# Longer planned delays for the recurrence's steps, and a rearranged tail, in a three-branch mixer layer

## The chip, the core and the metric

The kernel runs on one core of a Trainium2 chip. It is one launch, and the metric is the device time of that launch in microseconds (us), the median of several runs. A core has a matrix engine (TensorE, PE; its weight loads are PEld), three elementwise engines (VectorE, DVE; ScalarE, ACT; GpSimd, POOL), and SyncE (SP), from whose queue this kernel issues its DMA transfers. Each engine takes its instructions in the order in which the program has them; semaphores make one engine wait for another.

## The reference

One layer of a diffusion backbone on 256 latent tokens and 256 context tokens, width 2048; only the latent stream is returned.

```python
h = rms_norm(x) * (1 + scale) + shift                  # context and latent rows, (512, 2048)
(na_q, na_k, na_v, na_gate, pool_u, pool_gate, rw_r, rw_k, rw_v, rw_gate,
 rw_lw, rw_la, merge_logits) = split(h @ w_in)         # w_in: 2048 x 16512
y_na   = neighbourhood_attention(q, k, v, k_ctx, v_ctx, rpb)    # 16 heads of 64
y_pool = multiscale_pool(pool_u)                       # windows 2, 4, 8, 16
y_rw   = rwkv7 over context, then latents, both directions      # 16 heads of 64
def step(S, inp):                                      # the recurrence of one head
    S = S * w + (S @ a) b^T + v k^T;  y = S @ r
b_i = y_i * silu(gate_i)                               # three branches, 1024 wide
merged = sum_i sigmoid(merge_logits_i) * (b_i @ w_branch[i])
out = rms_norm(x + gate * (merged @ w_out)) * final_g
```

All is float32. The kernel makes each large product from two halves of each operand, high and low, in three matmuls.

## The kernel before

**Stages.** First come the modulation, the norm and the first column tiles of `w_in` ("start"). Then a long mixed stage runs everything up to the branch products. The last stage ("out", matmuls named `o`) multiplies by `w_out`, adds the residual and stores.

**Filler work.** The mixed stage draws its large matmuls from units. A column tile (line L815, accumulator `d`) multiplies `h`, held in `hh0..15` and `hl0..15` (high and low), with 128 columns of `w_in`. A merge group (L582 to L584, accumulator `dg`) computes 512 columns of merge logits; there are 12, each of 8 units. A branch group (also `dg`) computes 512 columns of one branch's product in 4 units; there are 12: branches 0 (attention), 1 (pool) and 2 (recurrence), four each. Each unit loads one `raw` tile of weights (three buffers, L564); ACT casts its halves (`whi`, L576) and DVE subtracts the rest (`wlo`, L577). Entries of the list `todo` carry the name of an event that must have happened; merge groups carry none and so fill whatever is left.

**Small streams.** Beside the units run generators: attention and pooling (`side`), and `rwkv(p)` for each of eight head pairs p (two heads of 64; called "head p" from here on). A head goes through these steps:

- `features`, for q = 0 (context) and q = 1 (latents): matmuls `psw`, `psa`, `psn`, and much elementwise work that ends in the tile `BK` (L210, L211)
- `scores`: transposes `pv`, copied by ACT to `SV` (L235); transposes `pt` (L242) of `BK`, copied by ACT to `BKT` (L244); products `pb` and `pk` (L257, L259), masked by DVE into `AT` and `EO` (L277)
- `inverse`: the triangular blocks go through DRAM (`dA`, `iA`, `dT`, `AT`), 31 steps on DVE, and `merge`: DVE transposes `DN` (L335), matmuls `mp` (L339, L347)
- `chain`: eight chunk steps, each `px` (L374), then `pu` (L388), copied to `SV` (L390), then `pS` (L398)
- `readout`: `pm`, `pvv`, a square root, a reciprocal; then the gate `grwg`, and `keep`, which splits the result (`kh`, L843, and L845) and writes it to `bs` in DRAM (L846, L847)

`branch_load(i)` reads 256 rows of `bs` back as `bh{i}` and `bl{i}` (L623) into the place of `hh{i}`, `hl{i}`: i = 0 to 3 for attention, 4 to 7 for pool, 8 to 11 for the recurrence. The modulation's own gate is computed in 64 small loads `wg` (L1070) with matmuls `mg` (L1082), taken one at a time beside the units once attention and pooling have ended (`side7`).

**What sets the order.** The class `Order` keeps a planned clock `t`. A generator yields a pair: the planned PE time of what it has just issued, and a delay; it is taken up again when `t` has passed the delay, and filler units go in between. PE's instructions stand in just the order that this planning gives. The other engines' orders are set by the framework's scheduler. A longer delay issues nothing: it puts more filler matmuls between two steps.

```python
s.t += r[0]
x[1] = (s.t if r[0] else min(x[1], s.t)) + r[1]     # when the stream may go on
```

## Time and profile before

| | |
|---|---|
| median of 3 runs | 1622.84 us (1619.48 to 1625.39) |
| the profiled execution | 1622.48 us; its span, first to last instruction, 1620.7 us |
| mean granted clock of TensorE | 0.980 |
| HBM read, written | 265.38 MB, 21.50 MB |
| chain of work that ended last | PE 57%, DMA 6%, DVE 4%, ACT 3% of the span |

The profile is of one execution. In its rows, "PE pt L242 <- DVE BK L210: 7.0, 3, 2.9" says that PE sat idle before a `pt` of line 242 until DVE's `BK` of line 210 was done: 7.0 us in total, three times, the longest 2.9. Busy shares are means over stages with different limits, so the prediction goes by stages. "Clock" is the share of full speed that TensorE was granted.

### The profile page before, as it was taken

The page shows a single profiled execution, that of the slowest core. Times are in us where ns is not written, and L with a number is a line of the kernel's source. Part 1 is how long each engine was busy: PE and PEld are TensorE (multiplying, and loading weights), DVE is VectorE, ACT ScalarE, POOL GpSimd, SP SyncE. Part 2 cuts the span into 40 slices and gives each one's busy share as a digit, 9 for nine tenths or more (in the row PEclk, how much of TensorE's full clock was granted, in tenths as well). Part 3 has the DMA queues.
Part 4 walks back from the last instruction along what each step waited for, and adds up shares of the span by engine and source line. Part 5 has one row for each costly group of instructions (what it writes and reads, how often), then busy time and mean ns, then how long its engine had stood idle before and what let it go on. Part 6 is the DMA issues. An engine that isn't in the chain of part 4 may idle for free.

```text
span 1620.7 us, 32318 instructions
## 1 busy us (share of the span) xinstructions
PE 1532.6 (95%) x12280; PEld 1219.3 (75%) x12280; DVE 1125.8 (69%) x2566; ACT 809.4 (50%) x1603; POOL 241.9 (15%) x441
## 2 busy tenths in 40 slices
PE   6999989989999998998999999999898997999998
PEld 4667778778777887876887798788687664667787
DVE  4234887898787788778867778886786542556674
ACT  5224753674565465456445646645643342334553
POOL 2222100330130041031013014102203200000000
PEclk9999999999999999999999999999999998999999
DMA  9997355345443444622532554443265678899862
GB/s 375 331 331 235 121 161 169 119 140 163 118 134 104 141 148 137 182 94 80 180 118 81 157 158 126 139 128 110 63 198 170 191 253 281 286 288 307 284 234 103
DMA packets 218380, 289.26 MB, mean 178 GB/s; under 512 B 62576, under 2 KB 176368, under 8 KB 213616
## 3 DMA queue, kind: packets, MB, share of 16 engines
q1 hardware_dynamic: 218224, 287.20, 54.8%
q8 instruction: 96, 1.57, 0.4%
q14 instruction: 60, 0.49, 0.1%
HBM read 265.38 MB, written 21.50 MB: 177 GB/s over the span
## 4 chain that ended last, share of the span: by engine, by line
PE 57%; DMA 6%; DVE 4%; ACT 3%; issue 1%; SPq 0%; ACTq 0%; DVEq 0%
PE d L815 24%; PE dg L582 6%; PE dg L583 5%; PE dg L584 5%; PE o L582 2%; PE o L584 2%; PE o L583 2%; DMA raw<-in_w_br 2%; PE pu L388 1%; DMA wg<-in_w_mg 1%; PE px L374 1%; DMA bh<-bs 1%; PE pS L398 1%; PE mg L1082 1%; DVE wlo L577 1%
## 5 line engine op out<-in xcount | busy, mean ns | idle before, releaser
L576 ACT CAST whi<-raw 128x512 fp32r<-128x512 f32 x584 | 354.8, 619 | 420.3 <-PE d L815 188.8
L577 DVE TENSOR_TENSOR wlo<-raw,whi 128x512 fp32r<-128x512 f32 x584 | 401.3, 700 | 191.0 <-ACT whi L576 147.7
L815 PE MATMUL d<-hh,whi 128*128 128x256 f32 (+1 forms) x1184 | 370.5, 332 | 0.0
L815 PE MATMUL d<-hl,whi 128*128 128x256 f32 (+1 forms) x1184 | 360.7, 324 | 0.0
L815 PEld LDWEIGHTS d<-hh,whi 128*128 128x128 f32 x1184 | 226.5, 191 | 23.2 <-issue 1.8
L815 PE MATMUL d<-hh,wlo 128*128 128x256 f32 (+1 forms) x1184 | 243.0, 325 | 0.0
L815 PEld LDWEIGHTS d<-hl,whi 128*128 128x128 f32 x1184 | 226.9, 192 | 17.1 <-issue 0.9
L815 PEld LDWEIGHTS d<-hh,wlo 128*128 128x128 f32 x1184 | 184.0, 192 | 16.8 <-issue 0.7
L582 PE MATMUL dg<-whi,hh 128*128 128x512 f32 x384 | 165.8, 432 | 6.3 <-ACT whi L576 2.2
L584 PE MATMUL dg<-wlo,hh 128*128 128x512 f32 x384 | 152.7, 398 | 1.9 <-DVE wlo L577 1.9
L583 PE MATMUL dg<-whi,hl 128*128 128x512 f32 x384 | 152.7, 398 | 0.0
L370 POOL TENSOR_SCALAR sg<-SV,G 64x64 f32<-64x64 f32 x192 | 108.2, 569 | 225.6 <-DVE SV L405 128.9
L582 PEld LDWEIGHTS dg<-whi,hh 128*128 128x128 f32 x384 | 73.0, 190 | 30.4 <-issue 6.3
L582 PE MATMUL dg<-whi,bh 128*128 128x512 f32 x192 | 81.6, 425 | 8.3 <-ACT whi L576 4.7
L584 PEld LDWEIGHTS dg<-wlo,hh 128*128 128x128 f32 x384 | 73.4, 191 | 19.5 <-DVE wlo L577 2.7
L583 PEld LDWEIGHTS dg<-whi,hl 128*128 128x128 f32 x384 | 73.5, 191 | 10.6 <-issue 0.2
L584 PE MATMUL dg<-wlo,bh 128*128 128x512 f32 x192 | 76.4, 398 | 0.5 <-DVE wlo L577 0.5
L583 PE MATMUL dg<-whi,bl 128*128 128x512 f32 x192 | 76.2, 397 | 0.0
L309 DVE TENSOR_TENSOR iM<-iA,iT 128x126 f32<-128x126 f32 (+22 forms) x248 | 65.7, 265 | 8.4 <-DMA iA<-dA 2.4
L311 DVE TENSOR_TENSOR iT<-iT,iM 128x126 f32<-128x126 f32 (+22 forms) x248 | 65.7, 265 | 6.1
L748 ACT ACTIVATE hh<-xT,md 128x256 fp32r<-128x256 f32 x32 | 17.5, 593 | 90.9 <-DVE md L705 90.9
L582 PEld LDWEIGHTS dg<-whi,bh 128*128 128x128 f32 x192 | 36.6, 191 | 29.4 <-ACT whi L576 11.7
(323 smaller groups left out, 2514.9 us busy)
## 6 DMA issues: line engine op xcount, KB each, us to landing
raw<-in_w_in SPq DMA_DIRECT2D x244, 512.0 KB, 3.5
wm<-in_w_ms SPq DMA_DIRECT2D x32, 1024.0 KB, 6.8
raw<-in_w_br SPq DMA_DIRECT2D x48, 512.0 KB, 6.0
wg<-in_w_mg SPq DMA_DIRECT2D x64, 256.0 KB, 5.4
raw<-in_w_out SPq DMA_DIRECT2D x32, 512.0 KB, 4.3
wst<-in_w_st SPq DMA_DIRECT2D x16, 448.0 KB, 7.5
md__79<-mth SPq DMA_DIRECT2D x24, 256.0 KB, 3.0
bth<-md__79 SPq DMA_DIRECT2D x24, 256.0 KB, 3.8
```

The lines of the kernel that those rows point to most:

```text
L309: nc.vector.tensor_tensor(m, A[:, st:st + 1, st + 1:32].to_broadcast([128, ni, nt]), T[:, 0:ni, st:st + 1].to_broadcast([128, ni, nt]), AL ...
L311: nc.vector.tensor_tensor(T[:, 0:ni, st + 1:32], T[:, 0:ni, st + 1:32], m, ALU.add)
L370: nc.gpsimd.tensor_scalar(sg[hv[par], d], SV[hv[par], par, w, d], G[hv[par], gs[d][0], d:d + 1], None, ALU.mult)
L374: nc.tensor.matmul(px[hv[par], d], EO[:, par, d, cs[d], :], SV[:, par, w, d], start=True, stop=True, tile_position=(0, 64 * par))
L388: nc.tensor.matmul(pu[hv[par], d], AT[hv[par], cs[d], d, :], xs[hv[par], d], start=True, stop=True)
L576: nc.scalar.copy(hi, src)
L577: nc.vector.tensor_tensor(lo, src, hi.bitcast(F32), ALU.subtract)
L582: nc.tensor.matmul(acc, a[0], b[0], start=start, stop=False)
L583: nc.tensor.matmul(acc, a[1], b[0], start=False, stop=False)
L584: nc.tensor.matmul(acc, a[0], b[1], start=False, stop=stop)
L748: nc.scalar.activation(hh[j][:, c], xT[:, j, c], AF.Identity, bias=mds[j][:, e:e + 1], scale=mds[j][:, 2 + e:3 + e])
L815: nc.tensor.matmul(box[0], w[m >= 8][:, 128 * i:128 * i + 128], x, start=(v == 0 and m == 0), stop=(v == 3 and m == 11))
```

## The change

It has four parts.

1. Longer delays. Old and new, in planned us: after `psw`, `psa` 1.6 to 2.2; before `kk` 3.6 to 4.4; after `BK` 3.6 to 5.2 (q = 0) and 4.8 to 6.6 (q = 1); after `pv` 1.2 to 2.4; after `pt` 1.6 to 2.4; after each pair of `pb`, `pk` 2.6 to 3.4; after `DN` 2.8 to 4.4; after `mp` 1.8 to 2.4 and 1.6 to 2.2; after `px` 1.2 to 1.6 (q = 0) and 0.7 to 1.0 (q = 1); after `pu` 1.6 to 2.0; after `pS` 1.8 to 2.0 and 1.9 to 2.2; after `pm` 4.0 to 5.0.
2. The gate of head 7 (`rwg7`) may be computed once attention of head 7 has ended (event `at7`), into the buffer `g2n` of attention's gates; before, it waited for head 6's result and used `g2r`.
3. The last entry of `todo`, merge group 11, is held back until it is the only one.
4. The loads of branch inputs 0 to 7 go out one pair at a time, at units 5, 6, 7, 8, 10, 12, 14 and 16 counted from that last group's start, where before two pairs went out at each of units 4 to 7. Those of the recurrence go one at a time from unit 18 on, once head 7 is done. The gates' loads come with two of three halves of a unit (before: one of two), but not during units 4 to 8.

```diff
             (nc.scalar.copy if par else nc.vector.tensor_copy)(SV[hv[par], par, w], pu[hv[par]])
-            yield 0.4, 1.6
+            yield 0.4, 2.0
...
-            todo.append((f"rw{p - 1}" if p else None, gate_(RW_G + p, f"rwg{p}", "g2r")))
+            if p < 7:
+                todo.append((f"rw{p - 1}" if p else None, gate_(RW_G + p, f"rwg{p}", "g2r")))
+            else:
+                todo.append(("at7", gate_(RW_G + p, f"rwg{p}", "g2n")))
...
                             i = next((i for i, (ev, _) in enumerate(todo) if ev is None or O.has(ev)), None)
+                            if i is not None and i == len(todo) - 1 and todo[:-1]:
+                                i = None
...
                         if last is not None:
-                            for i in (2 * last - 8, 2 * last - 7):
-                                if 0 <= i < 8:
-                                    branch_load(i)
-                            if last >= 10 and loads and O.has("rw7"):
-                                branch_load(loads.pop(0))
+                            if last in (5, 6, 7, 8, 10, 12, 14, 16):
+                                branch_load(last - 5 if last < 9 else last // 2 - 1)
+                            if last >= 18 and loads and O.has("rw7"):
                                 branch_load(loads.pop(0))
                             last += 1
...
-                    if n % 2 and O.has("side7") and gates:
+                    if n % 3 and O.has("side7") and gates and not 4 <= (last or 0) < 9:
                         ready[-1] = ready[-1] + gates.pop(0)()
```

What that does to the order, at three places. First PE, from head 7's last `pt` of its context half to its first `pb`. In the names, `d15` is a column tile and `dg0` a merge group, `pu6_4` the fifth chain step of head 6. Before:

```order
L242 MATMUL pt7_0_1_13997<-ident_63,BK7_0_13728 128x64
L388 MATMUL pu6_4_14016<-xs6_4_13989,AT6_1_12707 64x64 x4
L815 MATMUL d15_13896<-hh8_89,whi593_13892 128x512
L815 MATMUL d15_13896<-hl8_105,whi593_13892 128x512
L815 MATMUL d15_13896<-hh9_90,whi593_13892 128x512
L815 MATMUL d15_13896<-hl9_106,whi593_13892 128x512
L815 MATMUL d15_13896<-hh10_91,whi593_13892 128x512
L815 MATMUL d15_13896<-hl10_107,whi593_13892 128x512
L257 MATMUL pb7_0_0_14035<-EO7_0_13947,BK7_0_13728 64x64 x2
```

The same stretch of PE now:

```order
L242 MATMUL pt7_0_1_15135<-ident_63,BK7_0_14839 128x64
L582 MATMUL dg0_15058<-whi689_15054,hh2_83 128x512
L583 MATMUL dg0_15058<-whi689_15054,hl2_99 128x512
L584 MATMUL dg0_15058<-wlo689_15055,hh2_83 128x512
L388 MATMUL pu6_4_15165<-xs6_4_15127,AT6_1_13626 64x64 x4
L582 MATMUL dg0_15058<-whi690_15062,hh3_84 128x512
L583 MATMUL dg0_15058<-whi690_15062,hl3_100 128x512
L584 MATMUL dg0_15058<-wlo690_15063,hh3_84 128x512
L582 MATMUL dg1_15106<-whi689_15054,hh2_83 128x512
L583 MATMUL dg1_15106<-whi689_15054,hl2_99 128x512
L584 MATMUL dg1_15106<-wlo689_15055,hh2_83 128x512
L257 MATMUL pb7_0_0_15182<-EO7_0_15080,BK7_0_14839 64x64 x2
```

Nine large matmuls stand in the gap where six stood, and the filler is a merge group: the place has moved from among the column tiles to the tail.

Second SP's queue around the loads of branch inputs. Before (`raw` are the weights of a unit, `wg` those of the modulation's gate):

```order
L623 DMA bh4_16303<-bs_80 128x2x256
L623 DMA bl4_16305<-bs_80 128x2x256
L623 DMA bh5_16307<-bs_80 128x2x256
L623 DMA bl5_16309<-bs_80 128x2x256
L1070 DMA wg1_0_4_16315<-in_w_mg 128x2x256
L564 DMA raw730_16337<-in_w_in 128x4x256
L623 DMA bh6_16339<-bs_80 128x2x256
L623 DMA bl6_16341<-bs_80 128x2x256
L623 DMA bh7_16343<-bs_80 128x2x256
L623 DMA bl7_16345<-bs_80 128x2x256
L1070 DMA wg1_0_5_16351<-in_w_mg 128x2x256
L564 DMA raw733_16369<-in_w_br 128x4x256
```

SP's queue now, at inputs 5 and 6:

```order
L623 DMA bh5_16081<-bs_80 128x2x256
L623 DMA bl5_16083<-bs_80 128x2x256
L1070 DMA wg1_1_4_16089<-in_w_mg 128x2x256
L564 DMA raw748_16123<-in_w_br 128x4x256
L1070 DMA wg1_1_5_16129<-in_w_mg 128x2x256
L1070 DMA wg1_1_6_16139<-in_w_mg 128x2x256
L924 DMA bth0_1_0_16159<-md__79 128x512
L924 DMA bth0_1_1_16161<-md__79 128x512
L564 DMA raw751_16163<-in_w_br 128x4x256
L623 DMA bh6_16165<-bs_80 128x2x256
L623 DMA bl6_16167<-bs_80 128x2x256
```

Between two tiles of weights stood two pairs of branch inputs; now one pair, and two tiles lie from one pair to the next.

Third SP's queue where head 7's result is written (`kh2_7`, `grwg7`) and read back. Before:

```order
L623 DMA bh1_16238<-bs_80 128x2x256
L1089 DMA gb0_16182<-in_rows 128x512
L846 DMA bs_80<-kh2_7_16200 128x256
L847 DMA bs_80<-grwg7_14999 128x256
L623 DMA bl1_16240<-bs_80 128x2x256
L1070 DMA wg1_0_2_16246<-in_w_mg 128x2x256
```

SP's queue there now (`raw838` belongs to the last unit of the first recurrence branch group, `raw841` to the next group):

```order
L564 DMA raw838_17441<-in_w_br 128x4x256
L1089 DMA gb3_17340<-in_rows 128x512
L1061 DMA gd_78<-gb3_17340 128x512
L924 DMA bth2_0_0_17411<-md__79 128x512
L1216 DMA gate_17857<-gd_78 128x512
L846 DMA bs_80<-kh2_7_17364 128x256
L847 DMA bs_80<-grwg7_13812 128x256
L924 DMA bth2_0_1_17413<-md__79 128x512
L564 DMA raw841_17467<-in_w_br 128x4x256
L623 DMA bh11_17443<-bs_80 128x2x256
L623 DMA bl11_17445<-bs_80 128x2x256
```

Head 7's result was written while branch inputs 1 and 2 were being loaded, with all twelve branch groups to come; now it is written after the weights of the first recurrence group, directly ahead of the load (`bh11`) that needs it.

## The prediction

> **What bounds the kernel now.** I read the engine totals first, then the busy time by stage, then what TensorE waited for in each stage, and last the clock around those waits. Engine totals from the page:

> ```profile
> PE 1532.6 (95%) x12280; PEld 1219.3 (75%) x12280; DVE 1125.8 (69%) x2566; ACT 809.4 (50%) x1603; POOL 241.9 (15%) x441
> ```

> TensorE (PE) runs 95% of the span of 1620.7 us, and no other engine comes near. Its instruction stream is the same 12280 matmuls after the change, so only its pauses and its slow-clock time can go. Busy time in four stages (length, then PE, PEld, DVE, ACT, POOL, clock, DMA share, GB/s):

> ```profile
> 150.00:560.00 410.00, 391.82 (x3482) 327.75 (x3481) 328.94 (x770) 230.21 (x476) 56.73 (x128) 0.99 0.46 143
> 560.00:1260.00 700.00, 669.74 (x6063) 553.86 (x6062) 551.92 (x1324) 383.28 (x782) 133.00 (x250) 0.98 0.43 133
> 1260.00:1510.00 250.00, 235.35 (x1271) 162.12 (x1271) 124.92 (x223) 93.82 (x168) 10.62 (x20) 0.97 0.84 271
> 1510.00:1620.00 110.00, 101.34 (x495) 84.57 (x493) 67.66 (x118) 50.71 (x101) 0.00 (x0) 0.98 0.58 199
> ```

> PE is idle 18 + 30 us up to 1260 us, where the recurrence runs, and 15 us in the tail of merge and branch groups, where the DMA engines are 84% busy. The waits of PE between 150 and 1260 us (us in total, times, longest):

> ```profile
> PE pt L242 <- DVE BK L210: 7.0, 3, 2.9
> PE pk L259 <- DVE EO L277: 6.3, 5, 1.8
> PE mp L339 <- DVE DN L335: 6.0, 3, 4.9
> PE pb L259 <- ACT BKT L244: 4.5, 1, 4.5
> PE pS L398 <- ACT SV L390: 4.4, 4, 1.5
> PE pt L242 <- ACT SV L235: 4.0, 5, 1.5
> PE pt L242 <- ACT BK L211: 2.8, 4, 1.0
> PE pk L259 <- ACT BKT L244: 2.3, 2, 1.7
> PE dg L584 <- DVE wlo L577: 1.9, 1, 1.9
> PE dg L582 <- DVE gnag L855: 1.9, 1, 1.9
> ```

> The first eight rows, 37.3 us in 27 waits, are recurrence steps that PE reached too early; each is preceded by a delay that the change lengthens. A wait costs more than itself: the clock falls around it. Stretches around the eight places up to 1260 us with a reduced clock, first four and last shown with the sum:

> ```profile
> 353.00:360.00 7.00, 4.91 (x54) 4.47 (x58) 5.82 (x12) 4.80 (x9) 0.00 (x0) 0.76 0.60 200
> 364.00:370.00 6.00, 4.19 (x43) 3.88 (x42) 5.91 (x13) 1.62 (x3) 0.00 (x0) 0.72 0.49 160
> 609.00:616.00 7.00, 5.60 (x52) 5.13 (x53) 6.34 (x13) 2.92 (x6) 5.84 (x11) 0.76 0.24 82
> 757.00:766.00 9.00, 5.47 (x53) 3.68 (x57) 5.46 (x14) 3.71 (x9) 0.00 (x0) 0.62 0.25 80
> ...
> 1235.00:1244.00 9.00, 7.35 (x124) 6.60 (x126) 3.72 (x8) 1.50 (x3) 0.00 (x0) 0.62 0.53 149
> sum 59.00, PE 43.10 PEld 36.19 DVE 42.11 ACT 24.92 POOL 8.34; mean PE 5.39 PEld 4.52 DVE 5.26 ACT 3.12 POOL 1.04
> ```

> Five stretches like the first lose 1.7 us of full clock each (7.00 x 0.24), three like 757:766 lose 3.4: 18.7 us, of which up to 15.9 us (59.00 - 43.10) may fall on time when PE was idle anyway. So between 2.8 and 18.7 us; I take 9, since the waits mostly come before the drop.

> [...]

> **The longer delays.** They issue nothing: they put more large matmuls (0.23 us each, below) between a recurrence step and the next. Counted in the order with the trace's durations, the work from pv to pt grows in all 16 cases by 0.5 to 2 us, from pt to pb in 15, as the quoted order shows for one. What each saves:
> - pt after BK and the second half of BK: 7.0 + 2.8 us. Ahead of it stand +0.6, +0.8, +1.6 or 1.8, and +1.2 us. A single case is at most 2.9 + 1.0, so all 9.8 go.
> - pt after SV (L235): five waits up to 1.5, +1.2 each: 3.7 of 4.0.
> - pb and pk after BKT: +0.8 here and +1.2 a step earlier, which lets ACT drain: 2.0 of 4.5 and 1.6 of 2.3.
> - pk after EO: five waits up to 1.8, +0.8 each: 4.0 of 6.3.
> - pS after SV: four waits, +0.4 each: 1.6 of 4.4.
> - mp after DN: +1.6 covers the two short ones (1.1) and 1.6 of the 4.9: 2.7 of 6.0.
> Together 25.4 of 37.3 us; bounds 12 (half of it re-forms elsewhere) and 37. Two thirds of the clock loss of 9 goes with it: 6. The two dg rows are waits of filler work and stay. Waits that were short by chance of the order remain the least certain thing here.

> **Moved work.** Before, head 7's last chain steps end 150 merge matmuls behind the first gate matmul (mg); now head 6's whole chain and all of head 7 but its first feature matmuls stand behind it, and head 7's readout 621 behind it. So the tail of 250 us at 84% DMA gets more PE work for the same bytes, and the stages ahead get less vector work. I book no gain of its own for that; it makes the next term safer.

> **Branch inputs and gates.** Waits of PE in the tail, 1260 to 1510 us; its weight transfers (KB, us to landing); ACT's wait for them over the span; and the clock around the worst place:

> ```profile
> PE dg L582 <- ACT whi L576: 6.9, 4, 3.8
> PE dg L582 <- DVE bth L929: 2.6, 5, 0.9
> ...
> PE mg L1082 <- DMA wg<-in_w_mg: 1.7, 2, 1.3
> ```

> ```profile
> raw<-in_w_br SPq DMA_DIRECT2D x48, 512.0 KB, 6.0
> ...
> raw<-in_w_in SPq DMA_DIRECT2D x17, 512.0 KB, 3.4
> ```

> ```profile
> ACT whi L576 <- DMA raw<-in_w_br: 74.4, 35, 6.0
> ```

> ```profile
> 1343.00:1350.00 7.00, 5.74 (x21) 3.13 (x19) 1.40 (x3) 1.73 (x4) 0.00 (x0) 0.76 0.73 232
> 1360.00:1374.00 14.00, 9.24 (x25) 5.07 (x25) 3.79 (x7) 3.41 (x6) 0.00 (x0) 0.63 0.84 272
> ```

> The casts that dg waits for (whi) themselves wait for weights that stand in SP's row behind eight pairs of branch loads. Spread over units 5 to 16 one pair stands between two weight tiles, so 6.9 + 1.7 = 8.6 us go. The two stretches lose 1.7 + 5.2 us of clock, with 6.0 us of PE idle in them: I take 4. Together 12, bounds 0 and 15. That the gates' loads come in two of three halves, not one of two, is paid by their pause while branch loads run. The gate tile in attention's buffer costs nothing: the same four steps of filler, only earlier.

> **The end of head 7.** Its readout is now followed by one group and a half before its result is needed. Before, 519 dg matmuls stand between its last readout matmul and the first use of bh11; now 51. The readout before (start us, us), and landings of bs (by the rows of kh) and of bh:

> ```profile
> 1313.30 0.28 PE L109 MATMUL pvv<-yv,bones 128*128 128x256 f32 x1
> ...
> 1313.42 0.39 PE L582 MATMUL dg<-whi,hh 128*128 128x512 f32 x1
> ...
> 1313.65 0.40 PE L583 MATMUL dg<-whi,hl 128*128 128x512 f32 x1
> ```

> ```profile
> 1320.66 0.42 DVE L845 TENSOR_TENSOR grwg<-grwg,kh 128x256 fp32r<-128x256 f32 x1
> ```

> ```profile
> 1322.96 0.38 SPq L847 DMA_DIRECT2D bs<-grwg  x1
> ```

> ```profile
> DMA to landing us min/median/max: 3.3/3.3/3.3
> ```

> ```profile
> DMA to landing us min/median/max: 3.5/5.9/8.1
> ```

> From pvv's end (1313.6) to bs landed (1322.96 + 3.3 = 1326.3) is 12.7 us; bh11 and bl11 then take 3.5 to 8.1, say 5, as the queue is short there: 17.7. PE's cover is 51 x 0.23 = 11.7 plus about 1.2 of gate matmuls: 12.9. The wait is 4.8 (bounds 3.3 and 7.9), plus 1.7 of clock: -6.5. Behind bs in SP's row stand the next group's weights, which arrive with bh11. Head 7's inverse now lies in the tail too: four transfers in a row at 6.0 instead of 3.4 us would be 10 us late, less 1.6 and what its vector work gains from the freer DVE; I charge 4 (bounds 0 and 9).

> **Sum.** 25.4 + 6 + 12 - 6.5 - 4 = 33 us off the profiled 1622.48 us (span 1620.7 and 1.8 around it; the median of the runs is 1622.84): 1589.6, so 1590.

> **Rivals.**
> - The transfers set the tail (0.09): at 271 GB/s and 84% the branch and gate loads still come late, the 12 us stay: 1602. Against it: more PE time for the same bytes.
> - The waits re-form (0.08): ACT and DVE work in order, and a step that comes later meets another cast; DVE is 79% busy from 560 to 1260 us. Then the 31 us stay and only the tail moves: 1621, no change. Against it: the pt, pk and pb waits recur at the same step with the same size, which is a missing distance rather than a chance.
> - SP's row blocks the weights (0.09, slower). Waits in SP's row over the span:

> ```profile
> SPq L846 <- ACT kh L843: 55.8, 21, 6.2
> ...
> SPq L288 <- DVE SV L405: 22.7, 7, 7.2
> ```

> Heads 6 and 7 now put six such transfers among the tail's weights. Three raw buffers cover 8.2 us of PE work; a hold of 7.2 plus a landing of 6.0 plus a cast and subtraction of 1.3 is 14.5, 6.3 too long. Six times that with 1.7 of clock each is 48: 1638. It decides from 5.5 us each; today's mean hold is 2.7 to 3.2 us, under the cover.

> **How the numbers follow.** Likeliest 0.74 at 1590, its own range 1574 to 1606 from the bounds above. 1602 lies inside it, 1621 and 1638 outside; leaving out the last and most of the re-formed waits gives 1572 to 1614. This kernel's measurement tells 0.3% (4.9 us) from no change: faster 0.83, same 0.08, slower 0.09.

> **What would show it.** In the new profile the eight recurrence rows should sum to about 12 us instead of 37; reduced-clock stretches before the tail should be three or four, not eight; dg after whi in the tail should be under 2 us; a new wait of dg for bh11 of 3 to 8 us should stand 156 dg matmuls (36 us) ahead of the out stage, with a clock dip. I am wrong if the recurrence rows keep over 25 us, or if the tail shows waits of several us for raw behind dA, dT or bs transfers.

## The result and the profile after

The changed kernel takes 1573.87 us (median of 4 runs, 1569.64 to 1578.32) against 1621.16 us for the kernel before: a ratio of 0.9706, with a 95% interval of 0.9671 to 0.9741. The forecast was 1590 in a range from 1572 to 1614: faster, as said, but by 47 us where 33 were booked. The profiled execution has a span of 1572.6 us (1620.7 before) and a granted clock of 0.991 (0.980 before).

Engine totals from the page of after (busy us, share of the span, instructions):

```profile
PE 1514.0 (96%) x12280; PEld 1204.3 (77%) x12280; DVE 1125.0 (72%) x2566; ACT 799.2 (51%) x1597; POOL 244.0 (16%) x441
```

TensorE runs the same 12280 matmuls in 18.6 us less busy time (1532.6 before). Nearly all of that is the clock: by the trace's clock records, which grant a share of 1.0 or of 0.5 and nothing else, the time at half clock fell from 65.5 to 30.4 us, and half of the difference is 17.5 (in after, 128x512 matmuls in a row start 0.228 us apart at full clock and 0.427 at half). The span fell by 48.1, so the other 29.5 us are pauses. The first subtraction on this page already splits the gain into two parts, and shows which of them was forecast too small.

By stages, cut at the first column tile, the first gate matmul `mg` and the first `o`. Columns: length, busy PE, PEld, DVE, ACT, POOL, clock, DMA share, GB/s. Before:

```profile
150.10:1261.90 1111.80, 1063.36 (x9556) 882.78 (x9554) 882.31 (x2095) 614.63 (x1258) 191.35 (x379) 0.98 0.44 137
1261.90:1521.20 259.30, 244.65 (x1313) 170.12 (x1310) 132.00 (x235) 97.94 (x177) 8.90 (x17) 0.97 0.85 274
```

After:

```profile
148.40:1190.00 1041.60, 1021.59 (x8939) 849.48 (x8939) 817.16 (x1906) 575.21 (x1184) 168.46 (x336) 0.99 0.46 144
1190.00:1473.80 283.80, 269.07 (x1931) 189.07 (x1930) 196.39 (x424) 128.46 (x246) 33.94 (x59) 0.98 0.81 259
```

Ahead of the first gate matmul PE paused 48.4 us (length less busy time) and now pauses 20.0. In the tail it paused 14.7 us and still does, although 618 matmuls have moved into it. So all of the idle time that went, 28.4 us, went from the stretch with the recurrence. The waits of PE there, after, between 150 and 1230 us (us in total, times, longest):

```profile
PE pS L398 <- ACT SV L390: 3.3, 3, 1.8
PE dg L582 <- DVE gnag L855: 2.3, 3, 1.2
PE S L1000 <- DVE gnag L1029: 2.1, 1, 2.1
PE dg L582 <- DVE grwg L855: 1.8, 1, 1.8
PE nv L989 <- ACT vt L874: 1.7, 1, 1.7
PE mp L339 <- DVE DN L335: 1.6, 2, 1.1
PE dg L582 <- DVE gplg L855: 1.6, 1, 1.6
PE pk L259 <- DVE EO L277: 1.5, 1, 1.5
...
PE pt L242 <- ACT SV L235: 0.2, 1, 0.2
```

Of the eight recurrence rows that the prediction added to 37.3 us, four are left with 6.6 us here, and 8.1 us with the tail's (`pS` 1.3, `pk` 0.2). The rows of `BK` and `BKT` are gone. Five rows belong to other streams, 9.5 us together: filler matmuls `dg` that wait for the gates' work of attention, recurrence and pool (gnag, grwg, gplg), and attention's own matmuls `S` and `nv`. In the tail, from 1230 to 1470 us:

```profile
PE dg L582 <- ACT whi L576: 7.6, 4, 4.2
PE dg L582 <- DVE sum L929: 2.1, 1, 2.1
PE dg L582 <- DMA bh<-bs: 1.3, 1, 1.3
PE pS L398 <- ACT SV L390: 1.3, 2, 1.1
```

The row of whi, which the change was to take away, is 7.6 us where it was 6.9. The new wait for `bh11` is 1.3 us, not 4.8.

### The profile page after: what moved, and what is told of

Read it like the earlier page. It is cut to its first block, busy times and chain, and to the rows that moved or that the text cites. A ratio compares the mean times of both kernels' runs of the same rounds, so it can differ in the third digit from the quotient of the medians.

```text
span 1572.6 us, 32331 instructions
## 1 busy us (share of the span) xinstructions
PE 1514.0 (96%) x12280; PEld 1204.3 (77%) x12280; DVE 1125.0 (72%) x2566; ACT 799.2 (51%) x1597; POOL 244.0 (16%) x441
## 4 chain that ended last, share of the span: by engine, by line
PE 82%; DVE 6%; DMA 6%; ACT 3%; issue 2%; SPq 1%; ACTq 0%; POOL 0%; DVEq 0%; POOLq 0%
PE d L815 31%; PE dg L582 8%; PE dg L583 7%; PE dg L584 6%; PE acc L735 2%; PE psm L685 2%; PE o L582 2%; PE o L584 2%; PE o L583 2%; DMA raw<-in_w_br 2%; DVE wlo L577 2%; PE acc L741 2%; PE acc L738 2%; PE px L374 1%; PE pu L388 1%
## 5 line engine op out<-in xcount | busy, mean ns | idle before, releaser
L576 ACT CAST whi<-raw 128x512 fp32r<-128x512 f32 x584 | 355.9, 619 | 400.2 <-PE d L815 173.8
L577 DVE TENSOR_TENSOR wlo<-raw,whi 128x512 fp32r<-128x512 f32 x584 | 401.1, 697 | 142.2 <-ACT whi L576 105.9
L815 PEld LDWEIGHTS d<-hl,whi 128*128 128x128 f32 x1184 | 226.1, 191 | 16.3 <-issue 0.2
L582 PE MATMUL dg<-whi,hh 128*128 128x512 f32 x384 | 164.9, 429 | 5.7 <-DVE gnag L855 2.3
L583 PE MATMUL dg<-whi,hl 128*128 128x512 f32 x384 | 151.7, 395 | 0.0
L584 PE MATMUL dg<-wlo,hh 128*128 128x512 f32 x384 | 151.2, 394 | 0.1
L582 PEld LDWEIGHTS dg<-whi,hh 128*128 128x128 f32 x384 | 72.6, 189 | 29.5 <-issue 5.5
L582 PE MATMUL dg<-whi,bh 128*128 128x512 f32 x192 | 84.0, 437 | 11.6 <-ACT whi L576 7.6
L584 PEld LDWEIGHTS dg<-wlo,hh 128*128 128x128 f32 x384 | 72.7, 189 | 17.1 <-DVE wlo L577 0.6
L583 PEld LDWEIGHTS dg<-whi,hl 128*128 128x128 f32 x384 | 73.0, 190 | 9.8
L584 PE MATMUL dg<-wlo,bh 128*128 128x512 f32 x192 | 77.2, 402 | 0.5 <-DVE wlo L577 0.5
L583 PE MATMUL dg<-whi,bl 128*128 128x512 f32 x192 | 76.9, 400 | 0.2 <-DMA bl<-bs 0.2
L748 ACT ACTIVATE hh<-xT,md 128x256 fp32r<-128x256 f32 x32 | 17.5, 594 | 89.4 <-DVE md L705 89.4
L582 PEld LDWEIGHTS dg<-whi,bh 128*128 128x128 f32 x192 | 37.0, 193 | 30.1 <-ACT whi L576 11.8
## 6 DMA issues: line engine op xcount, KB each, us to landing
raw<-in_w_in SPq DMA_DIRECT2D x244, 512.0 KB, 3.5
raw<-in_w_br SPq DMA_DIRECT2D x48, 512.0 KB, 5.1
raw<-in_w_out SPq DMA_DIRECT2D x32, 512.0 KB, 4.3
```

What stands on the lines that cost most here:

```text
L576: nc.scalar.copy(hi, src)
L577: nc.vector.tensor_tensor(lo, src, hi.bitcast(F32), ALU.subtract)
L582: nc.tensor.matmul(acc, a[0], b[0], start=start, stop=False)
L583: nc.tensor.matmul(acc, a[1], b[0], start=False, stop=False)
L584: nc.tensor.matmul(acc, a[0], b[1], start=False, stop=stop)
L815: nc.tensor.matmul(box[0], w[m >= 8][:, 128 * i:128 * i + 128], x, start=(v == 0 and m == 0), stop=(v == 3 and m == 11))
```

## Experiments

Three theories were set against each other. A: each longer gap takes away the waits behind it, and some slow clock with each wait. B: the rearranged tail (parts 2 to 4) gives the gain. C: what matters is only that heads 6 and 7 come later.

The table holds all runs. "Stage" is the mixed stage from the first column tile to the first `o` in the profiled execution, "idle" its length less PE's busy time, "half" its time at half clock, summed from the trace's clock records. The last column is stage − idle − half / 2, what would be left without pauses at full clock.

| kernel | median us | ratio to before [95%] | stage | idle | half | left |
|---|---|---|---|---|---|---|
| before | 1621 to 1625 | 1 | 1371.1 | 63.1 | 54.6 | 1280.7 |
| after | 1573.87 | 0.9706 [0.9671, 0.9741] | 1325.4 | 34.7 | 23.9 | 1278.7 |
| 1 delays alone | 1585.83 | 0.9767 [0.9742, 0.9791] | 1336.4 | 42.6 | 34.1 | 1276.8 |
| 2 tail alone | 1615.79 | 0.9954 [0.9932, 0.9976] | 1368.6 | 61.1 | 51.2 | 1281.9 |
| 3 shift by 16 | 1593.34 | 0.9815 [0.9786, 0.9844] | 1340.9 | 45.7 | 30.7 | 1279.8 |
| 4 old loads | 1577.76 | 0.9718 [0.9689, 0.9747] | 1331.5 | 36.9 | 34.1 | 1277.5 |
| 5 features, scores | 1580.21 | 0.9751 [0.9718, 0.9784] | 1328.3 | 37.7 | 17.1 | 1282.1 |
| 6 merge, chain | 1603.99 | 0.9888 [0.9863, 0.9914] | 1355.7 | 55.0 | 34.1 | 1283.6 |
| 7 shift by 8 | 1602.62 | 0.9881 [0.9854, 0.9909] | 1355.9 | 53.2 | 27.3 | 1289.0 |
| 8 rows by POOL | 1577.75 | 0.9727 [0.9702, 0.9751] | 1327.8 | 38.0 | 20.5 | 1279.6 |
| 9 BK's delay old | 1568.81 | 0.9659 [0.9644, 0.9674] | 1323.0 | 30.7 | 23.9 | 1280.4 |
| 10 longer still | 1592.49 | 0.9806 [0.9775, 0.9837] | 1349.7 | 49.5 | 44.4 | 1278.0 |
| 11 after, again | 1574.76 | 0.9682 [0.9665, 0.9700] | 1330.9 | 36.6 | 30.7 | 1278.9 |
| 12 old loads, again | 1578.87 | 0.9712 [0.9695, 0.9730] | 1324.2 | 36.1 | 17.1 | 1279.5 |

The last column is the main finding. It lies between 1277 and 1284 us in all rows but one (kernel 7, 5 us above). In nearly every order the work itself takes the same time, and the length of the stage is this constant plus PE's pauses plus half of the half-clock time. From before to after the stage lost 45.7 us: 28.4 of pauses, 15.4 of clock (half of 30.7) and 2.0 in the last column.

**1. The delays alone** (part 1; parts 2 to 4 put back).

```diff
-                            if last in (5, 6, 7, 8, 10, 12, 14, 16):
-                                branch_load(last - 5 if last < 9 else last // 2 - 1)
+                            for i in (2 * last - 8, 2 * last - 7):
+                                if 0 <= i < 8:
+                                    branch_load(i)
...
```

> The longer delays alone; the gate of head 7, the held-back group, the branch loads and the gates' loads are as before. Theory A (the gain is the recurrence's waits of PE, and the clock they cost, taken away by the longer distances): about 1582 us, 0.972 to 0.980 of before, with the eight recurrence rows near 7 us as in the changed kernel instead of 37, and half-clock time up to the first gate matmul near 14 us instead of 37; what is missing against the changed kernel (1574) is the tail. Theory B (the gain is mostly the rearranged tail): 1605 us or more, 0.99 of before. Theory C (the gain is that heads 6 and 7 moved into the tail, where there is room): also about 1580, since the delays alone move them as far; the shift kernel tells A from C.

1585.83 us: the delays alone give 2.3 of the 2.9%. B is out. Its trace is as A has it: the eight recurrence rows are 7.8 us (37.3 before), and half-clock time up to the first gate matmul is 13.7 us (37.5 before). Most of what separates it from the changed kernel stands in its tail, where PE pauses 19.2 us (14.7 in the changed kernel) and runs 20.5 us at half clock (10.2). The waits of PE from 1187 to 1300, 1300 to 1340 and 1400 to 1490 us:

```profile
PE dg L582 <- DMA bh<-bs: 5.6, 1, 5.6
...
PE mg L1082 <- DMA wg<-in_w_mg: 4.6, 2, 3.3
...
PE dg L582 <- DMA bh<-bs: 5.0, 1, 5.0
```

These three rows are 15.2 us that the changed kernel has not or hardly has (1.3): with the heads late, the old tail starts a branch group at once with `bh0` (issued at 1289.15 us, while PE waits from 1289.1) and runs into `bh11` with too little in between.

**2. The tail alone** (parts 2 to 4; delays put back).

```diff
-        yield 0.0, (5.2 if q == 0 else 6.6)
+        yield 0.0, (3.6 if q == 0 else 4.8)
...
```

> The rearranged tail alone (gate of head 7 in attention's buffer, held-back group, spread branch loads, denser gates); all delays as before. Theory A: the recurrence's waits stay at about 37 us and the time is 1612 to 1621, 0.995 to 1.0 of before; the tail's own waits of 14.5 us may fall by half. Theory B: 1590 or less, 0.98 of before. Theory C: as before, within 0.5%, since the heads stay where they were (head 7's last readout matmul even earlier).

1615.79 us, 0.5%: as A has it. It removes 2.0 us of pauses and 3.4 of half clock. Gains of 2.3% and 0.5% add up to nearly the 2.9% of the whole.

**3. A shift at one place** (as 2, with one delay in `inverse` 16 us longer, so that everything behind it comes later).

```diff
-        yield 0.0, 10.5
+        yield 0.0, 26.5
```

> The rearranged tail, the delays as before, and 16 us added to each head at one place alone, the delay after the inverse's transfers (10.5 to 26.5), so that heads 6 and 7 come as late as in the changed kernel (head 7's last readout matmul 591 large matmuls behind the first gate matmul, against 621) while the gaps between the other steps stay short. Theory A: the pt, pk, pb and pS waits stay (25 to 31 us in those rows), only mp after DN goes (6 us) and the time is 1605 to 1616. Theory C: most of the gain without the longer gaps, 1580 to 1590, with the waits gone because ACT and DVE are less crowded.

1593.34 us, between the two. Against 2 its waits at `pt` fell from 13.8 to 5.0 us although no delay there is longer, while those at `pk` rose from 7.9 to 10.8. So A in its strict form does not hold: another order of the same steps takes some waits away by itself. **7**, the same with 8 us, asked how much lateness is enough:

> As the shift kernel (delays as before, the rearranged tail, an added delay at one place), with 8 us for each head instead of 16: head 7's last readout matmul stands 315 large matmuls behind the first gate matmul. If lateness itself takes the waits away, about half of the 22 us between the tail alone (1616) and 16 us of shift (1593): 1602 to 1607, with about 27 us of recurrence waits. If those waits went because the steps happened to meet other work in that one order, no such rule: the sum of waits can be that of either, 1590 to 1618, and does not fall with the shift.

1602.62 us, in the window of C, but with 18.0 us of recurrence waits and not 27; the rival without a rule (1590 to 1618) allows it too, so this run does not decide. With the delays as before, the time falls the later the heads come: 1615.79 us in 2, 1602.62 in 7 and 1593.34 in 3, where head 7's last readout lies 75, 315 and 591 large matmuls behind the first gate matmul. So C holds a part of the truth. Kernel 7 also left a remainder of 1289.0 us, which the table's sum does not explain.

**5 and 6. One half of the delays each**, with the new tail. In 5 the delays of `features` and `scores` are long, in 6 those of `merge`, `chain` and `readout`.

Kernel 5 against the changed kernel, first place:

```diff
-        yield 0.0, 4.4
+        yield 0.0, 2.8
...
```

and kernel 6:

```diff
-        yield 1.0, 2.2
+        yield 1.0, 1.6
...
```

> The rearranged tail, and the longer delays in the features and scores alone (psw, kk, BK, pv, pt, pb and pk); those of merge, chain and readout as before. Heads 6 and 7 move about half as far (head 7's last readout matmul 198 large matmuls behind the first gate matmul; 75 with the new tail alone, 621 in the changed kernel). Theory A (waits go where the gap is longer): the pt, pk and pb waits of 27 us fall under 5 and the time is 1580 to 1590, while pS and mp keep 8 us. Theory C (waits go because the heads come later): as in the next kernel, which moves them equally far, both 1598 to 1608.

> The rearranged tail, and the longer delays in merge, chain and readout alone; those of features and scores as before. Heads 6 and 7 move as far as in the kernel with the scores' delays (225 against 198 large matmuls). Theory A: pt, pk and pb keep 20 us or more of waits, pS and mp fall, and the time is 1604 to 1616, clearly over that kernel. Theory C: the same time as that kernel.

1580.21 and 1603.99 us. Head 7's last readout lies 198 large matmuls behind the first gate matmul in 5 and 225 in 6 (75 in the tail alone, 621 in the changed kernel): nearly equally late, 24 us apart. So longer gaps are worth something that lateness alone does not give, which speaks for A against C. But A is not right in detail: in 6 the waits of `pt`, `pk` and `pb` are 12.3 us where it expected 20 or more. Waits of PE in 6 from 150 to 1510 us:

```profile
PE pt L242 <- ACT BK L211: 5.0, 5, 1.4
...
PE pb L257 <- ACT BKT L244: 2.7, 2, 2.0
PE pt L242 <- ACT SV L235: 2.7, 2, 1.4
```

and in 5, where the largest are

```profile
PE dg L582 <- ACT whi L576: 6.6, 4, 2.4
PE dg L582 <- DVE gplg L855: 4.1, 2, 3.9
PE S L1000 <- DVE gnag L1029: 3.1, 2, 2.1
PE pvv L108 <- ACT yv L102: 2.9, 5, 0.9
```

In 5 only 3.9 us are left of the waits of pt, pk, pb, mp and pS, fewer than in the changed kernel (8.5), though `mp` and `pS` kept their old delays; A expected 8 us of those two. The delays of features and scores carry most of the gain (36 of 42 us against the tail alone).

**9. One delay put back**, the largest of the four that the prediction's largest single item (9.8 us of `pt` after `BK`) rests on.

```diff
-        yield 0.0, (5.2 if q == 0 else 6.6)
+        yield 0.0, (3.6 if q == 0 else 4.8)
```

> The changed kernel with one delay put back, the one after BK (5.2 to 3.6 us in the context half, 6.6 to 4.8 in the latent half). Head 7's last readout stays 582 large matmuls behind the first gate matmul (621 with the change), so the head is as late as in the changed kernel. Theory A (each longer gap takes away the waits behind it, and with each wait some slow clock): the waits of pt for BK come back, 6 to 10 us, and 4 to 8 half-clock stretches of 3.4 us with them, of which half is lost: 1585 to 1596. Theory C (what matters is that heads 6 and 7 come later): pt's waits for BK stay under 3 us, and the time within 0.3% of the changed kernel's, 1570 to 1578.

1568.81 us, by its median faster than the changed kernel on the same chip (1574.76), though the intervals of the two ratios overlap a little; that it beats the changed kernel is likely and not shown. Neither A's 1585 to 1596 nor its waits came: no wait of `pt` for `BK` is left, and the one row of `pt` in the stage is

```profile
PE pt L242 <- ACT SV L235: 1.4, 1, 1.4
```

The trace says why. For the 16 context and latent halves I took, from the instructions of L230, L242 and L211, the time from the first `pv` to the first `pt`, and to the end of `BK`'s last piece:

| kernel | pv to pt, shortest | mean | latest BK after pv | halves in which the first pt starts ahead of BK's last piece |
|---|---|---|---|---|
| before | 2.2 us | 3.0 | 6.8 | 4 |
| 6 merge, chain | 2.2 | 2.5 | 4.3 | 6 |
| 9 BK's delay old | 3.5 | 3.7 | 3.5 | 0 |
| after | 3.2 | 3.6 | 2.7 | 0 |

The delay after `pv` (1.2 to 2.4) widens the gap from `pv` to `pt`, and `BK` is done inside it. The delay after `BK` stands ahead of `pv`: it makes `BK` earlier against `pv` (2.7, not 3.5 us), but that was no longer needed. Two delays in a row covered one wait. The opposite, the delay after `pv` put back alone, was not run.

**10. Two delays longer still**, for the rows that are left.

```diff
-            yield 0.4, 2.0
+            yield 0.4, 2.6
...
-            yield 1.3, 3.4
+            yield 1.3, 4.0
```

> The changed kernel with two delays longer still: after pu 2.0 to 2.6, after each pair of pb and pk 3.4 to 4.0. Theory A: the waits of pS for SV (4.6 us) and of pk for EO (1.7 us) go, with one or two half-clock stretches: 5 to 9 us less, 1565 to 1569. Rival (what is left is no missing distance, and the waits move to filler work or to other steps): 1571 to 1577, with the two rows smaller and others larger by as much.

1592.49 us: slower than the changed kernel by 18 us, outside both expectations. The waits of `pk` for `EO` are gone and `pS` is down to 1.6 us, but the new order has others (PE, 150 to 1510 us):

```profile
PE dg L582 <- DVE gnag L855: 7.9, 6, 2.1
PE dg L582 <- ACT whi L576: 6.9, 6, 3.3
PE po L1028 <- ACT PT L1019: 3.8, 2, 2.6
PE px L374 <- DVE SV L405: 3.8, 4, 2.0
PE dg L582 <- DMA bh<-bs: 3.1, 1, 3.1
```

Pauses rose by 14.7 us and half-clock time by 20.5 against after's profile. That is the prediction's rival "the waits re-form", here for a further lengthening. Which of the two delays did it was not run apart. The first gate matmul stands at 1260 us, nearly where it was before the change (1190 after): the streams fell into another order, and a gap that is long enough for its own step says nothing on the waits of the others.

**4 and 12. The old rule for branch loads** in the changed kernel, the second time beside the changed kernel itself (**11**) on one chip.

```diff
-                            if last in (5, 6, 7, 8, 10, 12, 14, 16):
-                                branch_load(last - 5 if last < 9 else last // 2 - 1)
-                            if last >= 18 and loads and O.has("rw7"):
+                            for i in (2 * last - 8, 2 * last - 7):
+                                if 0 <= i < 8:
+                                    branch_load(i)
+                            if last >= 10 and loads and O.has("rw7"):
+                                branch_load(loads.pop(0))
...
```

> The changed kernel with the loads of branch inputs put back to two pairs at each of units 4 to 7 and those of the recurrence from unit 10 on, two at a time; everything else, the denser gates and the longer delays too, as changed. If spreading the loads is worth the 8.6 us of waits and 4 us of clock that the prediction booked: 1584 to 1587 against 1574. If it is worth nothing, as the unchanged sum of the tail's waits (14.5 us before and after) suggests: 1572 to 1577, with the same sum of waits in the tail.

> The changed kernel itself, on the chip and against the same runs as the other three: 1570 to 1578, ratio 0.968 to 0.974.

> The changed kernel with the old rule for loading branch inputs, as before, now beside the changed kernel on one chip and in more rounds. If the spreading is worth what the prediction booked (8.6 us of waits and 4 of clock), 10 to 13 us more than the changed kernel; if it is worth what the one profile showed (3 us of idle time and half of 10 us of slow clock), 4 to 8; if that was the scatter between executions, under 3 us.

1577.76 against 1573.87 us, and 1578.87 against 1574.76 on one chip: 4 us both times, with intervals that overlap. The spread loads are worth about that (any gain at all is likely and not shown), not 12. The traces of 4 and 12 show the place that the prediction described. In 12 a tile of weights is issued at 1277.77 us behind two pairs of branch loads (from 1275.55 on) and lands at 1284.14. PE waits for it, and 6.8 us at half clock follow; in 4 the wait is 3.1 us, with 6.8 at half clock. The wait in 12 (150 to 1300 us):

```profile
PE dg L582 <- ACT whi L576: 4.6, 1, 4.6
```

With the spread loads the longest such wait ahead of 1300 us is 1.1 us (after), and 11 has none. The profiles do not give the net gain: the profiled execution of 12 fell among its fastest, and 11's took 6.5 us longer in its span than after's, the same program. Of that, 1.9 us are pauses and 3.4 half of the additional slow clock (30.7 against 23.9): these two executions of one program differ mostly by where the clock drops.

**8. The gate's rows by POOL's queue.** In the changed kernel SP issued no weights for 12.9 us in the tail. SP's queue there (start us, us):

```profile
1300.85 0.55 SPq L564 DMA_DIRECT2D raw<-in_w_br  x1
...
1307.34 0.34 SPq L1089 DMA_DIRECT2D gb<-in_rows  x1
...
1308.88 0.57 SPq L315 DMA_DIRECT2D dT<-iT  x1
...
1312.62 0.35 SPq L1061 DMA_DIRECT2D gd<-gb  x1
1313.07 0.57 SPq L315 DMA_DIRECT2D dT<-iT  x1
1313.73 0.66 SPq L564 DMA_DIRECT2D raw<-in_w_br  x1
...
1315.98 3.77 SPq L321 DMA_DIRECT2D AT<-dT  x8
...
1320.78 0.42 SPq L564 DMA_DIRECT2D raw<-in_w_br  x1
```

`gb` waits 4.8 us for `mg`, `gd` 2.1 for `gb`, and then come the eight transfers of head 7's inverse. Experiment 8 sends `gb` and `gd` from POOL's queue.

```diff
-            nc.sync.dma_start(gd[:, c], gb)
+            nc.gpsimd.dma_start(gd[:, c], gb)
...
```

> The changed kernel with eight transfers of the gate's bias rows and results (gb loads and gd stores, four each) issued from POOL's queue instead of SP's, so that they no longer hold the weight loads behind them. In the changed kernel no weight load was issued from 1300.9 to 1313.7 us while SP waited for gb and gd, and PE then waited 2.1, 1.6 and 4.2 us with 6.8 us at half clock. If that hold causes these waits: 7 to 11 us faster than the changed kernel, 1563 to 1567, ratio 0.964 to 0.967. If the transfers were late for bandwidth: no change, 1571 to 1577.

1577.75 us: no gain. The hold by `gb` and `gd` did shrink: no weights went out for 8.3 us ahead of 1310.24, where it was 12.9 ahead of 1313.73, and a wait of 1.6 us that ended at 1318.7 is gone. But the tail's longest wait is still there, 4.1 us from 1322.2 us, since the inverse's transfers still hold SP (kernel 8):

```profile
1301.91 0.56 SPq L564 DMA_DIRECT2D raw<-in_w_br  x1
...
1310.24 1.44 SPq L564 DMA_DIRECT2D raw<-in_w_br  x1
...
1314.84 4.45 SPq L321 DMA_DIRECT2D AT<-dT  x8
...
1320.30 0.42 SPq L564 DMA_DIRECT2D raw<-in_w_br  x1
```

The weights that this wait ends on went out at 1320.30 us, behind the eight transfers, and at 1320.78 in the changed kernel. There they landed at 1326.0, were cast by 1326.7, and `dg` started at 1326.8 after 4.2 us of waiting. So for the longest wait `gb` and `gd` were not the last thing to wait for; head 7's inverse was. This is read from the order of events: a run with those eight transfers elsewhere was not made. Other waits took what the earlier weights won; PE pauses 19.1 us in this tail (14.7 in after, 16.3 in 11).

## Why the prediction came out as it did

- **Recurrence waits: right in kind, too small in size.** 25.4 of 37.3 us were to go, 29.2 went (8.1 left). Item by item the working held less well. `pt` after `BK`: all 9.8 went, as booked; four delays were counted for it, and the one after `BK` was not needed (9). `pt` after `SV`: 3.8 of 4.0, booked 3.7. `pb` and `pk` after `BKT`: 6.8 of 6.8, booked 3.6. `pk` after `EO`: 4.6 of 6.3, booked 4.0. `mp`: 4.4 of 6.0, booked 2.7. `pS`: nothing of 4.4, booked 1.6. Counting how much each gap grows gives the sum within a fifth, but it treats steps as independent where a delay also decides how early the work ahead is done. Kernel 3 shows that a mere shift takes away 8.8 us at `pt`, so a part of the gain may be lateness and not the gaps; the runs do not split it.
- **Filler waits.** They were to stay. Ahead of the gate matmuls 30.7 us of recurrence waits went (37.3 to 6.6) and the pauses fell by 28.4, so other waits grew by 2.3.
- **Clock: the step that failed in size.** Booked were 6 us in the recurrence and 4 in the tail, less 1.7 at the end: 8.3. In the mixed stage 15.4 came: half-clock time fell from 37.5 to 13.7 us ahead of the gate matmuls (11.9) and from 17.1 to 10.2 in the tail (3.4). The page's busy time says 18.6 for the whole span. The wrong step is the 9 us taken out of bounds of 2.8 and 18.7 for the eight places. Its reason, that the waits mostly come before the drop, is true and speaks for the upper bound: only time that PE sat idle during the drop lessens the loss. The trace of before has 3.3 us of idle time in its 37.5 us at half clock, so the loss there was (37.5 - 3.3) / 2 = 17.1 us. Two thirds of it are 11.4, close to the 11.9 that came. Here is what is left, the stretches after with a reduced clock outside the out stage:

```profile
211.00:220.00 9.00, 6.91 (x18) 4.80 (x18) 7.66 (x19) 4.02 (x9) 0.03 (x1) 0.62 0.27 89
497.00:504.00 7.00, 5.20 (x29) 3.94 (x28) 4.88 (x13) 3.02 (x6) 0.91 (x5) 0.76 0.00 0
725.00:732.00 7.00, 5.41 (x75) 4.12 (x75) 3.47 (x7) 1.19 (x2) 0.11 (x1) 0.76 0.52 165
1322.00:1333.00 11.00, 6.76 (x23) 4.71 (x23) 3.11 (x5) 3.42 (x6) 0.00 (x0) 0.69 1.02 330
1431.00:1439.00 8.00, 6.48 (x21) 4.62 (x20) 3.67 (x6) 3.00 (x5) 0.00 (x0) 0.79 0.91 293
```

Three ahead of the tail, as forecast (three or four).

- **Tail: the term failed.** 12 us were booked for the spread loads; idle time in the tail is 14.7 us as before, the row of whi is 7.6 us where under 2 were forecast, and kernels 4 and 12 give the loads 4. The whi waits were put down to eight pairs of loads in front of the weights. That holds for one place near 1284 us in kernels 4 and 12. The longest whi wait after has another cause: SP's queue was held by head 7's inverse. All parts of the tail together are worth about 8 us without the longer delays (kernel 2) and about 10 to 12 with them (kernel 1 against after). That this is near the 12 booked is luck: without the new tail kernel 1 waits 15.2 us in three places that the prediction had not in its sum. Parts 2 and 3 and the denser gates were not run apart.
- **The end of head 7: right in kind, too dear.** The wait stands where it was put, followed by a dip of the clock (1431 to 1439), but it is 1.3 us and not 4.8, with a dip of 3.4 us at half clock: 3.0 instead of 6.5 (1.3 plus half of 3.4). `bh11` was issued at 1428.28 us, 11.2 us after the last `pvv` (1417.06), and landed 4.7 after (5 was taken). PE's cover was 14.8 us, not 12.9.
- **Head 7's inverse in the tail: within its bounds, wrong in place.** 4 us (0 to 9) were charged for `mp` coming late. No `mp` waits in the tail; the inverse's eight transfers delay the weights behind them, and `dg` waits 4.2 us from 1322.5, with 6.8 us of half clock: 7.6 us. This is the third rival in small, at one place and not six, and a sign that the prediction had named for being wrong (a wait of several us for raw behind such transfers).

In sum, the prediction booked 24.6 us of pauses (25.4 and 8 of the tail's 12, less 4.8 and 4 at head 7) and 8.3 of clock. There came 28.4 and 15.4. A further 4.4 us came where nothing was booked: 1.7 in the start, 0.7 in the out stage, 2.0 in the constant; kernel 11 shows that two executions can differ by 6. Together these are, within rounding, the 48.1 us by which the span fell. The 1.7 of the start fit one more drop of the clock: before has 3.4 us at half clock at 28 us, after has none there. That the pauses came out well is in part luck: in the tail the gain that failed to come and the charges that were too high cancelled (0.8 us more pauses booked, none measured). The clock was booked at about half of what came. The time, 1573.87 us, lies just inside the range given (1572 to 1614) and just under the likeliest case's own (1574 to 1606).

## What to carry to other kernels

Before sizing an edit that only reorders, split the stage into its constant, the pauses of the bound engine, and half of its half-clock time: here this sum held within a few us over 13 of 14 profiles, and says what an order can win at most (34.7 us of pauses and 12 of clock are left). A missing distance can be covered at any step between the producer and the consumer: look for the one gap that contains both; here a second one bought nothing (9 against after). A longer gap is not a safe direction: two delays that were right for their own steps cost 18 us through the waits of the others (10 against 11), so each set of delays has to be run.

## What the hardware showed beyond that

Half clock followed many short waits as well as the long ones. I joined PE's pauses of over 0.3 us that were less than 4 us apart, from 150 us on, in all 14 profiles, and counted those with a half-clock stretch within 4.2 us of their end:

| pause, us | pauses | with a half-clock stretch |
|---|---|---|
| under 1 | 208 | 0 |
| 1 to 1.5 | 99 | 6 |
| 1.5 to 2 | 69 | 34 |
| 2 to 3.5 | 50 | 34 |
| 3.5 and over | 25 | 25 |

Many pauses recur from kernel to kernel, so these are not 451 independent cases. But half clock followed 34 of the 69 pauses of 1.5 to 2 us, and half of the shortest stretch, 3.4 us, is 1.7 us more; it followed none of the 208 under 1 us, each of them 4 us or more from the next. In this kernel the waits above 1.5 us are the first to shorten or to split. The stretches in the mixed stage last 3.41, 6.83 or 10.24 us in before and after, and the column "half" of the runs' table holds whole multiples of 3.41 in all 14 profiles.

| idle in a slice, us | slices | next slice at half clock |
|---|---|---|
| under 1.2 | 5161 | 0 |
| 1.2 to 1.5 | 51 | 5 |
| 1.5 to 2 | 80 | 58 |
| 2 and over | 36 | 36 |

So in these traces the idle time inside one slice tells the cases apart better than the length of a pause. Of the 69 pauses of 1.5 to 2 us in the first table, 46 had 1.5 us or more inside one slice, and half clock followed 34 of them; the other 23 were split by a slice's edge, and it followed none. The grid lies differently in each execution (its offset from the first instruction is 1.4 us in after and 3.2 in 11, the same program). That one and the same pause is followed by half clock in one execution and not in the next would fit this, but was not shown on a single pause.
